# A hybrid decoder block on one core: the conv sums' accumulating DMAs read the stored tiles, and the means and the output projection get fixed places

## The chip, the cores and the metric

The kernel runs on one core of one Trainium2 chip. The time is device microseconds of one execution on that core; three runs of the kernel before are at hand. Beside them there is one profiled execution with its trace. Lower is better. Differences of about 0.3% can be told from none.

The engines by their names in the profile: PE multiplies matrices (PEld is its weight loads), DVE and ACT work on vectors, POOL is the general one, SP issues most of the DMA transfers. Each engine takes its instructions in order; a waiting instruction holds everything behind it on its engine. SP's and POOL's DMA issues wait in the same way.

## The reference

The block has S = 1024 positions, D = 1024 channels, 8 heads and a feed-forward width of 2816, all in float32. What matters of it:

```python
h = rms_norm(x, attn_norm_w)
q, k, v, u, g = jnp.split(h @ w_in, splits, axis=-1)
...                                        # differential attention over q, k, v
y_a = a.reshape(B, S, ATTN_WIDTH) @ w_proj_attn
u_a, u_b = jnp.split(u, 2, axis=-1)
c = causal_depthwise_conv(u_a * jax.nn.sigmoid(u_b), conv_w, conv_b)   # width 31
c = jax.nn.silu(layer_norm(c, conv_ln_w, conv_ln_b))                  # over the channels
y_b = c @ w_proj_conv
g_a, g_b = jnp.split(jax.nn.sigmoid(g + gate_b), 2, axis=-1)
x = x + (g_a * y_a + g_b * y_b) @ w_out
h = rms_norm(x, ffn_norm_w)
gt, up = jnp.split(h @ w_gate_up, 2, axis=-1)
x = x + (jax.nn.silu(gt) * up) @ w_down
```

The LayerNorm needs, at every position, the mean over all 1024 channels. The kernel gets the sum over the channels in two steps: the eight channel tiles of 128 channels are added up elementwise, and one matrix product with a constant tile adds over the 128 rows that are left.

## The kernel before

**Precision.** Each matrix product is made of three: both operands are split into a high part (a cast on ACT, `split_hi`, L120) and a low part (the rest, a subtraction on DVE, `split_lo`, L125), and high x high, high x low and low x high are added in PSUM (`mm3`, L168 to L170). So each weight tile of 128 x 1024 costs a DMA into a raw buffer, a cast and a subtraction before PE may use it.

**Stages.** One input projection makes Q, K, V, U and G. Attention works head by head; in its gaps PE computes gate columns (L168 to L170 on `pg`). The convolution runs on DVE in the background of all that. Behind attention come the LayerNorm, the projections of both branches, the gated merge, the output projection and the feed-forward part.

**The convolution.** `conv_taps(c)` lists the steps of channel tile c (128 channels x 1024 positions): the first tap on ACT (L576) writes `acc`, thirty taps on DVE (L582) add to it, one per step. There is one buffer `acc` (for the first four tiles a PSUM tile, copied into one SBUF buffer `done` at the end). After the last tap SP stores the tile to `c_d[c]` in DRAM (L588), and POOL issues a DMA that adds the same buffer to `cs_d` in DRAM (L590, `accum_op=ALU.add`); the first tile is stored there plainly (L592). The steps lie in a list `bg`, from which the other stages take so many at a time; `bg.until(0)` takes the rest.

**LayerNorm and what lies around it.** `ln_chunks(sb)` works on one half of the positions: SP loads the sums (`lns`, L1537) and the eight tiles (`cT_lo`), ACT and DVE split the sums into `lnmh` and `lnml`, two matmuls with `part` give the mean (L1545), then DVE subtracts it from each tile (L1551). It is a generator; `ln_both` walks through both halves, and `ln_step()` takes as many steps as the list `lnp` says, between column groups of the projection of the attention branch. That projection's first group, `o3`, is eight k-tiles x two columns x two halves in four PSUM banks; `ya_out` multiplies each bank with its sigmoid gate (L1618, DVE `gt`), and after that the bank is free for the next group. `early` (L1474) loads attention results back for it, `aTh` and `aTl` are their two parts.

**Output projection.** It runs as seven products of half size (`WSEVEN`, index z; j counts the four k-steps, i the four row tiles, each with three matmuls), whose operands are sums and differences of quarters of the weights, made by `wless` (L1750, DVE) and split by `wsplit`. After each product its four banks are added to the rows `xa` (L1824, DVE). A product's operand may be split ahead of time by `early_weights`. `norm2` (L1709 to L1717) normalizes rows that are complete, transposes them on PE (`tr`) and copies them back; `NORMS` says after which product and step this stands. Then the feed-forward part begins with the columns that `ws.plan` lists.

**What sets the order.** The program is written in one order, and a scheduler with a model of the engines' times then lists each engine's instructions; it may let an instruction slip ahead of others. `with after(ins)` keeps what is issued inside behind the instruction `ins` in that listing. Buffers come from pools with a fixed number of places; a new tile waits until the last reader of the old one is done.

## Time and profile before

| | us |
|---|---|
| three runs | 1749.77, 1753.22, 1754.83 |
| median of the runs | 1753.22 |
| the profiled execution's own time | 1750.81 |
| its span in the trace | 1749.0 |
| its mean granted TensorE clock | 0.998 |

The prediction is worked out against the profiled execution and carried over to the median. In the rows, a time at the left is the start in us from the span's beginning, then the duration, the engine, the line of the kernel, the operation, `out<-in` by the names in the program, the form, and in brackets how long the engine had stood before it and what ended that. Lists of waits say engine, line, what it waited for, and then total us, number of times, and the longest. Rows of windows give, after the length, the busy us (and instructions) of PE, PEld, DVE, ACT and POOL, the granted clock, the mean busy share of the 16 DMA engines, and GB/s.

### The profile page before, as it was taken

What the parts mean: (1) busy time and instruction counts of PE and PEld (TensorE: products, weight loads), DVE (VectorE), ACT (ScalarE), POOL (GpSimd) and SP (SyncE); (2) the same over time, 40 slices, a digit from 0 to 9 for tenths busy, and PEclk for the clock granted to TensorE, in tenths of its full rate; (3) what the DMA queues carried; (4) which work ended last, traced back from release to release, by engine and by line L of the source; (5) the groups of instructions that cost most, each with busy time, mean ns of one, the idle gap of its engine ahead of it and who ended that gap; (6) DMA issues with size and microseconds to landing.
All of it is one profiled execution on the core that took longest, in us unless ns stands there. A gap on an engine that the chain in (4) does not pass through costs nothing. (4 is left out here: it accounts for less than half of the span.)

```text
span 1749.0 us, 25887 instructions
## 1 busy us (share of the span) xinstructions
PE 1719.7 (98%) x9245; PEld 1480.1 (85%) x9245; DVE 1273.7 (73%) x2128; ACT 860.9 (49%) x1958; POOL 217.5 (12%) x207
## 2 busy tenths in 40 slices
PE   9999999999999999999899999999999999999999
PEld 7997889998998998988788877788888888888887
DVE  7575889797987888978587677866667666565554
ACT  5333335666777776755466324633333333333332
POOL 4987761000000000000000000000000000000000
PEclk9999999999999999999999999999999999999999
DMA  6343555334345344443873673235545544598663
GB/s 204 116 134 124 170 175 150 112 87 131 107 123 143 100 119 118 112 132 123 309 254 121 205 264 134 79 103 165 167 147 167 172 152 144 165 358 290 217 218 131
DMA packets 257765, 281.64 MB, mean 161 GB/s; under 512 B 16418, under 2 KB 178274, under 8 KB 257636
## 3 DMA queue, kind: packets, MB, share of 16 engines
q1 hardware_dynamic: 254352, 269.55, 47.7%
q0 software_dynamic: 2992, 9.39, 2.3%
q8 instruction: 73, 1.20, 0.3%
q10 hardware_dynamic: 292, 1.05, 0.2%
q14 instruction: 56, 0.46, 0.1%
HBM read 178.17 MB, written 85.50 MB: 151 GB/s over the span
## 5 line engine op out<-in xcount | busy, mean ns | idle before, releaser
L582 DVE SCALAR_TENSOR_TENSOR acc<-u,cw,acc 128x1023 f32<-128x1023 f32 (+14 forms) x240 | 303.9, 1266 | 17.1 <-ACT acc L576 14.7
L168 PE MATMUL pg<-whi,hT_hi 128*128 128x256 f32 x704 | 199.6, 285 | 2.0 <-ACT jk L787 2.0
L169 PE MATMUL pg<-wlo,hT_hi 128*128 128x256 f32 x704 | 200.4, 285 | 0.9 <-POOL wlo L131 0.9
L170 PE MATMUL pg<-whi,hT_lo 128*128 128x256 f32 x704 | 199.7, 284 | 0.0
L125 DVE TENSOR_TENSOR wlo<-draw,whi 128x1024 fp32r<-128x1024 f32 x75 | 91.8, 1224 | 85.6 <-ACT whi L120 78.1
L120 ACT CAST whi<-draw 128x1024 fp32r<-128x1024 f32 x75 | 79.1, 1055 | 129.5 <-PE acc L482 121.0
L168 PEld LDWEIGHTS pg<-whi,hT_hi 128*128 128x128 f32 x704 | 134.1, 191 | 4.6 <-ACT jk L787 2.7
L169 PEld LDWEIGHTS pg<-wlo,hT_hi 128*128 128x128 f32 x704 | 134.3, 191 | 3.0 <-POOL wlo L131 1.1
L170 PEld LDWEIGHTS pg<-whi,hT_lo 128*128 128x128 f32 x704 | 134.3, 191 | 1.2
L120 ACT CAST whi<-wraw 128x1024 fp32r<-128x1024 f32 x90 | 94.3, 1050 | 60.2 <-PE pg L169 26.4
L482 PE MATMUL acc<-wlo,whi 128*128 128x512 f32 x308 | 119.9, 389 | 0.0
L482 PE MATMUL acc<-whi,wlo 128*128 128x512 f32 x308 | 119.9, 389 | 0.0
L1282 ACT ACTIVATE E<-E,mn 128x640 f32<-128x640 f32 (+7 forms) x128 | 99.6, 779 | 39.5 <-DVE mn L1277 37.4
L168 PE MATMUL pg<-hT_hi,whi 128*128 128x512 f32 x288 | 114.8, 399 | 3.0 <-ACT jk L787 3.0
L170 PE MATMUL pg<-hT_hi,wlo 128*128 128x512 f32 x288 | 114.2, 397 | 0.0
L169 PE MATMUL pg<-hT_lo,whi 128*128 128x512 f32 x288 | 114.0, 396 | 0.0
L120 ACT CAST whi<-s 128x1024 fp32r<-128x1024 f32 x54 | 56.8, 1052 | 107.3 <-PE acc L967 101.1
L125 DVE TENSOR_TENSOR wlo<-wraw,whi 128x1024 fp32r<-128x1024 f32 x75 | 92.8, 1239 | 13.7 <-ACT whi L120 13.5
L1277 DVE CUSTOM_DVE_ANT_0 E<-sc,tb 128x512 f32<-128x512 f32 (+3 forms) x128 | 74.8, 588 | 31.5 <-PE pT L1314 15.1
L967 PE MATMUL acc<-h_hi,whi 128*128 128x512 f32 x240 | 93.4, 389 | 0.0
L967 PE MATMUL acc<-h_lo,whi 128*128 128x512 f32 x240 | 93.4, 389 | 0.0
L967 PE MATMUL acc<-h_hi,wlo 128*128 128x512 f32 x240 | 90.2, 389 | 0.0
(371 smaller groups left out, 4590.4 us busy)
## 6 DMA issues: line engine op xcount, KB each, us to landing
wraw<-in_w_gate_up_dram SPq DMA_DIRECT2D x44, 512.0 KB, 4.7
wraw<-in_w_in_dram SPq DMA_DIRECT2D x40, 512.0 KB, 4.5
qs<-qs SPq DMA_DIRECT2D x96, 128.0 KB, 2.3
wd<-in_w_down_dram SPq DMA_DIRECT2D x44, 256.0 KB, 3.1
tdT<-wd SPq DMA_DIRECT2D x88, 128.0 KB, 4.7
draw<-sdS SPq DMA_DIRECT2D x44, 256.0 KB, 4.0
draw<-tdT SPq DMA_DIRECT2D x44, 256.0 KB, 4.0
wraw<-in_w_in_dram SPq DMA_DIRECT2D x32, 256.0 KB, 3.3
```

The source lines that it names most:

```text
L120: act.copy(dst, src)
L125: last_lo[0] = dve.tensor_tensor(dst, src, f32(hi), op=ALU.subtract).ins
L168: pe.matmul(o, lh, rh, start=start, stop=False)
L169: pe.matmul(o, lh, rl, start=False, stop=False)
L170: last_mm[0] = pe.matmul(o, ll, rh, start=False, stop=stop).ins
L482: m = pe.matmul(o[s_][i][:], l_[:, ts], r_[:, 512:], start=start and j + y_ == 0, stop=j == n - 1 and y_ == 2, skip_group_check=not start,)
L582: dve.scalar_tensor_tensor(a_, us[c][:, : S - n], cw[:, c, t : t + 1], a_, op0=ALU.mult, op1=ALU.add)
L967: last_mm[0] = pe.matmul(o[:], a_[x_][:, k, :], b_[y_][:, k, :], start=start and k + x_ + y_ == 0, stop=k == 3 and x_ == 1, skip_group_che ...
L1277: dve.tensor_tensor_reduce(e[:, ks], o[:, :w], tb[:, S - nk + c0 : S - nk + c0 + w], 1.0, mn[:, j : j + 1] if c0 else 3.0e38, ALU.add, ALU ...
L1282: act.activation(e[:, :nk], e[:, :nk], AF.Exp, bias=mn[:, j : j + 1], scale=-1.0, accum_out=l[:, j : j + 1])
```

## The change

It has three parts.

First, the accumulating DMA of tile c reads the stored tile `c_d[c]` in DRAM instead of the buffer, in pieces of 1 KB (512 pieces of 256 elements instead of 128 of 1024), and is written at tap 15 of the next tile (behind DVE's last instruction there); the last tile's comes after the rest of the list.

Second, the LayerNorm's means: `ln_chunks` stops once more ahead of the mean's matmuls in the first half, and the step that issues them is written behind the seventh k-tile of the first group `o3`; the eighth k-tile's matmuls come after the last of them. The next step is placed behind the first gates.

Third, the output projection: every matmul of it comes after the one written before it; the weight sums of "22" and "S3" and their early splits are written at steps j == 1 of the fourth and j == 2 of the fifth product instead of at their starts; the loads of the first two gate/up columns are issued at the start of the sixth product; the norms of the third and fourth row tile are written one step later.

```diff
@@ ld_cols
-        def go():
-            raw = wraw()
+        raw = []
+
+        def load():
+            raw.append(wraw())
             nc.sync.dma_start(
-                raw[:].rearrange("p (k c) -> p k c", c=P),
+                raw[0][:].rearrange("p (k c) -> p k c", c=P),
...
+        def go():
+            if not raw:
+                load()
+            hi, lo = wsplit(raw[0], tiles)
...
+        go.load = load
         return [go]
@@ the convolution
+    def add_tile(c):
+        pool.dma_start(cs_d[:], c_d[c][:], accum_op=ALU.add, max_dma_last_dim=1024)
...
                     nc.sync.dma_start(c_d[c][:], acc[0][:])
-                    if c:
-                        pool.dma_start(cs_d[:], acc[0][:], accum_op=ALU.add)
-                    else:
+                    if c == 0:
                         nc.sync.dma_start(cs_d[:], acc[0][:])
+                if c > 1 and t == CW // 2:
+                    with after(last_of(mybir.EngineType.DVE)):
+                        add_tile(c - 1)
...
     bg.until(0)
+    add_tile(NKT - 1)
@@ the LayerNorm
+        if not sb:
+            yield
         for s_ in (s1h, s1l):
-            pe.matmul(mean[:], part[:], s_[:], start=s_ is s1h, stop=s_ is s1l)
+            last_mean[0] = pe.matmul(mean[:], part[:], s_[:], start=s_ is s1h, stop=s_ is s1l).ins
...
-        for z in (0, 1, 0, 0, 0, 1, 1, 0, 0, 0, 1, 1, 1, 1):
+        for z in (0, 0, 1, 0, 0, 0, 1, 1, 0, 0, 0, 1, 1, 1, 1):
...
-    lnp = [1, 3, 2, 2, 2, 2, 2, 9]
+    lnp = [1, 1, 3, 2, 2, 2, 2, 2, 9]
...
-                mm3(o3[c][sb][:], ...)
+                with after(last_mean[0]):
+                    mm3(o3[c][sb][:], ...)
+        if k == NKT - 2:
+            with after(last_mm[0]):
+                ln_step()
     for c in range(NE):
         ya_out(c, o3[c], g3[c])
-    ln_step()
+    with after(first_gates):
+        ln_step()
@@ the output projection
-    NORMS = {(5, 3): (0, 1), (6, 0): (2,), (6, 1): (3,)}
+    NORMS = {(5, 3): (0, 1), (6, 1): (2,), (6, 2): (3,)}
...
-        if z == 3:
-            for q in range(2):
-                room["22", q] = wraw()[:]
-            with after(last_lo[0]):
-                wless("22", "12", "S2")
-            for q in range(2):
-                early_weights("22", q, 2 * q)
-            wless("S3", "S4", "S3")
-        if z == 4:
-            for j in (2, 3):
-                early_weights("S3", j, 2 * j)
...
+            if z == 3 and j == 1:
+                for q in range(2):
+                    room["22", q] = wraw()[:]
+                with after(last_lo[0]):
+                    wless("22", "12", "S2")
+                    wless("S3", "S4", "S3")
+                for q in range(2):
+                    early_weights("22", q, 2 * q)
+            if z == 4 and j == 2:
+                for q in (2, 3):
+                    with after(last_lo[0]):
+                        early_weights("S3", q, 2 * q)
+            if z == 5 and j == 0:
+                with after(last_of(mybir.EngineType.SP)):
+                    for step in plain_first:
+                        step.load()
...
-                    with after(last_mm[0] if z == 6 else None), after(last_tr[0]):
+                    with after(last_mm[0]), after(last_tr[0]):
...
-                with after(last_mm[0]), after(last_add if z == 6 else None):
+                with after(last_mm[0]), after(last_add if z == 6 else None), after(norm_lo if z == 6 else None):
                     norm2(t_, r2[0], tr_first)
+                if z == 5:
+                    norm_lo = last_lo[0]
```

What stands in the engines' rows at three of the places follows. Numbers behind names tell tiles apart; they shift by one or two between the two programs.

POOL around the last tile's add, at the end of attention. Before:

```order
L1305 MEMSET pl_9598 128x128
L1304 MEMSET ph_9597 128x128
L590 DMA cs_d<-acc_8106 128x1024
L1305 MEMSET pl_9713 128x128
L1304 MEMSET ph_9712 128x128
L1512 MEMSET part 128x128
```

After:

```order
L1319 MEMSET pl_9598 128x128
L1318 MEMSET ph_9597 128x128
L1319 MEMSET pl_9712 128x128
L1318 MEMSET ph_9711 128x128
L579 DMA cs_d<-c_d_147 512x256
L1527 MEMSET part 128x128
```

The add has moved behind the last pair of memsets and reads the stored tile.

PE at the end of the first group `o3` (four banks `pg_`), where the mean's two matmuls stand (`lnmh`, then `lnml`); the next group is `pg_10229`. Before:

```order
L168 MATMUL pg_9986<-aTh_9763,whi_9632 128x512
L169 MATMUL pg_9986<-aTl_9769,whi_9632 128x512
L170 MATMUL pg_9986<-aTh_9763,wlo_9633 128x512
L1545 MATMUL mean_9954<-lnml_9956,part 128x512
L168 MATMUL pg_9988<-aTh_9763,whi_9776 128x512
L169 MATMUL pg_9988<-aTl_9769,whi_9776 128x512
L170 MATMUL pg_9988<-aTh_9763,wlo_9777 128x512
L168 MATMUL pg_10229<-aTh_9758,whi_9975 128x512
```

After, with the four banks' twelve matmuls of the eighth k-tile behind the means (the first ones shown):

```order
L169 MATMUL pg_9986<-aTl_9910,whi_9776 128x512
L170 MATMUL pg_9986<-aTh_9908,wlo_9777 128x512
L1564 MATMUL mean_9954<-lnmh_9955,part 128x512
L1564 MATMUL mean_9954<-lnml_9956,part 128x512
L168 MATMUL pg_9983<-aTh_9763,whi_9631 128x512
L169 MATMUL pg_9983<-aTl_9769,whi_9631 128x512
L170 MATMUL pg_9983<-aTh_9763,wlo_9632 128x512
L168 MATMUL pg_9984<-aTh_9763,whi_9631 128x512
```

The low half of the mean has gone from three matmuls before the group's end to twelve.

PE in the output projection, from the second product (banks `wo_11566` to `wo_11569`) to the third (`wo_11646` to `wo_11649`); `wo_11498` to `wo_11500` are banks of the first product's kind, used again by the fourth. Before:

```order
L1814 MATMUL wo_11569<-whi_11530,mTl_10793 128x512
L1814 MATMUL wo_11498<-whi_11650 128x512
L1814 MATMUL wo_11499<-whi_11650 128x512
L1814 MATMUL wo_11500<-whi_11650 128x512
L1814 MATMUL wo_11646<-whi_11570,mTh_10782 128x512
L1814 MATMUL wo_11646<-wlo_11571,mTh_10782 128x512
L1814 MATMUL wo_11646<-whi_11570,mTl_10788 128x512
L1814 MATMUL wo_11646<-whi_11570,mTh_10784 128x512
```

After:

```order
L1843 MATMUL wo_11569<-whi_11530,mTl_10793 128x512
L1843 MATMUL wo_11646<-whi_11570,mTh_10782 128x512
L1843 MATMUL wo_11646<-wlo_11571,mTh_10782 128x512
L1843 MATMUL wo_11646<-whi_11570,mTl_10788 128x512
L1843 MATMUL wo_11647<-whi_11570,mTh_10782 128x512
L1843 MATMUL wo_11647<-wlo_11571,mTh_10782 128x512
L1843 MATMUL wo_11647<-whi_11570,mTl_10788 128x512
L1843 MATMUL wo_11648<-whi_11570,mTh_10782 128x512
```

The three matmuls of the fourth product are gone from ahead of the third, and the third goes from bank to bank at each step instead of finishing one bank first.

More of the change, by code (lines that the diff above doesn't have):

```diff
@@ L295, in ld_cols @@
     def ld_cols(w, c0, tiles=wtiles):
-        def go():
-            raw = wraw()
+        raw = []
+        def load():
+            raw.append(wraw())
             nc.sync.dma_start(
-                raw[:].rearrange("p (k c) -> p k c", c=P),
+                raw[0][:].rearrange("p (k c) -> p k c", c=P),
                 w[:, c0 : c0 + P].rearrange("(k p) c -> p k c", p=P),
             )
-            hi, lo = wsplit(raw, tiles)
+        def go():
+            if not raw:
+                load()
+            hi, lo = wsplit(raw[0], tiles)
             return (
@@ L550 @@
     for f in range(NSTD):
-        ws.plan(ld_cols(wgu, f * P) + ld_cols(wgu, FF + f * P, *([fourth] if f == 1 else [])))
+        plain = ld_cols(wgu, f * P) + ld_cols(wgu, FF + f * P, *([fourth] if f == 1 else []))
+        ws.plan(plain)
+        if f == 0:
+            plain_first = plain
     cv_ctx = ExitStack()
@@ L1524 @@
     cT_lo = big.tile([P, NKT, S], F32R, tag="xlo", name="cT_lo")
+    last_mean = [None]
     def ln_chunks(sb):
@@ L1635 @@
                 cs = slice(sb * 512, (sb + 1) * 512)
-                mm3(o3[c][sb][:], w3[c][0][:, k, :], w3[c][1][:, k, :], aT_hi[k][:, cs], aT_lo[k][:, cs], k == 0, k == NKT - 1)
+                with after(last_mean[0]):
+                    mm3(o3[c][sb][:], w3[c][0][:, k, :], w3[c][1][:, k, :], aT_hi[k][:, cs], aT_lo[k][:, cs], k == 0, k == NKT - 1)
+        if k == NKT - 2:
+            with after(last_mm[0]):
+                ln_step()
     for c in range(NE):
         ya_out(c, o3[c], g3[c])
-    ln_step()
+    with after(first_gates):
+        ln_step()
     for c in range(NE, NKT):
```

## The prediction

> **What bounds the kernel now.** I read the page's busy times first, then PE's list of waits, then the rows of each wait, then who is late there.
>
> ```profile
> PE 1719.7 (98%) x9245; PEld 1480.1 (85%) x9245; DVE 1273.7 (73%) x2128; ACT 860.9 (49%) x1958; POOL 217.5 (12%) x207
> ```
>
> PE is busy for 1719.7 of 1749.0 us. The change takes no matmul away, so all that it can win lies in some 29 us in which PE stands, plus what the granted clock loses after a stand. The list of PE's waits (line, releaser: us in total, times, longest) gives the largest:
>
> ```profile
> PE pg L168 <- ACT jk L787: 4.9, 4, 3.0
> PE tr L1712 <- ACT xa L1717: 2.7, 1, 2.7
> PE pg L168 <- DVE gt L1618: 2.5, 1, 2.5
> PE wo L1814 <- ACT whi L120: 1.8, 1, 1.8
> PE sc L1275 <- DVE mn L1277: 1.5, 2, 1.2
> ...
> PE sc L1275 <- DMA ks<-klo: 1.3, 1, 1.3
> ```
>
> The first and the last two are in the attention stage, the third at the LayerNorm's means, the others in the output projection: the three places that the change touches.
>
> **Part 1, the accumulating DMAs.** The first tap of a channel tile (L576, on ACT) writes into the one buffer that the add of the tile before (L590) still reads. These rows give what ACT waits for, when the tile's store (L588) and the add (L590) are issued, and how long they take to land:
>
> ```profile
>   DMA cs_d<-acc: 6.9, 3
>   DMA cs_d<-done: 2.1, 1
> ...
> L588 SPq DMA_DIRECT2D c_d<-acc x4: 320/332/344, 406.5 to 824.8; - x4
> DMA to landing us min/median/max: 2.9/4.5/5.3
> ...
> L590 POOL DMA_DIRECT2D cs_d<-acc x4: 863/864/873, 406.7 to 825.1; - x4
> DMA to landing us min/median/max: 7.4/9.0/10.0
> ```
>
> Afterwards the add reads the stored tile, so the first tap waits for the store alone, 3 to 7 us sooner. What that is worth is read at the places. The dearest:
>
> ```profile
> 413.11 0.19 ACT L787 ACTIVATION_READ_ACCUMULATOR jk<-pg 128x1 f32 x1
> 416.16 1.24 ACT L576 ACTIVATE acc<-u,pvec,cw 128x1024 f32<-128x1024 f32 x1 [2.86 <-DMA cs_d<-acc]
> ...
> 420.10 0.80 PE L168 MATMUL pg<-hT_hi,whi 128*128 128x512 f32 x1 [2.98 <-ACT jk L787]
> ...
> 420.00:423.00 3.00, 2.90 (x7) 2.35 (x8) 3.00 (x9) 2.54 (x7) 0.00 (x0) 0.50 0.21 80
> ```
>
> ACT is free at 413.3. The store was issued at 406.5 and landed by 411.8 at the latest (5.3), so the wait of 2.86 goes entirely. It is what holds back the squares (L787) that free PE's bank: PE's 2.98 goes with it. The last row (window; PE, PEld, DVE, ACT, POOL busy; granted clock; DMA share; GB/s) shows the clock at 0.50 for the 3 us behind the stand, which loses another 1.5 us. This place: 4.5 us.
>
> The second place goes through two engines:
>
> ```profile
> ACT acc L576 <- DMA cs_d<-acc: 2.2, 1, 2.2
> ...
> 559.70 0.17 DVE L1289 RECIPROCAL rl<-l 128x2 f32<-128x2 f32 x1 [4.25 <-ACT E L1282]
> ...
> 569.26 0.47 PE L1275 MATMUL sc<-ks,qs 128*128 128x512 f32 x1 [1.34 <-DMA ks<-klo]
> 575.69 0.33 PE L1275 MATMUL sc<-ks,qs 128*128 128x128 f32 x1 [1.15 <-DVE mn L1277]
> ```
>
> ACT's 2.2 (until 557.0) makes the exponentials late, DVE stands 4.25, its klo is late, and the DMA from it and the scores behind it are what PE waits for. Both PE waits, 1.34 + 1.15 = 2.5 us, are smaller than or about as large as the 2.2 removed at the head; I take them whole. Of ACT's four waits two are left (6.9 + 2.1 - 2.9 - 2.2 = 3.9 us); PE shows only small stands behind them, so I price both at 1.0, between 0 and 3.9. Part 1 gives 4.5 + 2.5 + 1.0 = 8.0 us; ends 7.0 and 10.9.
>
> The add's own price: it moves behind a tap in the middle of the next tile, on POOL behind a pair of memsets. The next pair waits for PE, near the second place for this long:
>
> ```profile
> POOL pl L1305 <- PE pW L170: 16.8, 1, 16.8
> ```
>
> The add has 512 pieces instead of 128, so 0.86 us of issue becomes at most four times that, 3.5: hidden under 16.8, and 2.6 each if that cover were gone. Nothing on SP stands behind an add except at the last tile (below). But the placing of the rest is remade: the orders of PE differ from row 1039 on, so every small stand of the attention stage is dealt anew. I price that at 0, ends -3 and +3.
>
> **Part 2, the means, and the loads ahead of them.** The add of the last tile shares the DMA engines with loads that PE waits for. Rows of PE, then ACT's wait, then the window:
>
> ```profile
> 836.79 0.50 PE L168 MATMUL pg<-aTh,whi 128*128 128x512 f32 x1 [0.76 <-ACT aTh L120]
> 838.05 0.50 PE L169 MATMUL pg<-aTl,whi 128*128 128x512 f32 x1 [0.76 <-DVE aTl L125]
> 839.19 0.50 PE L168 MATMUL pg<-aTh,whi 128*128 128x512 f32 x1 [0.41 <-ACT sgg L626]
> ...
> ACT aTh L120 <- DMA early<-a_d: 4.3, 2, 2.2
> ...
> 836.00:843.00 7.00, 5.07 (x14) 3.48 (x14) 5.28 (x8) 5.78 (x13) 0.00 (x0) 0.76 0.55 187
> ```
>
> The three stands are 1.93 us, and a clock of 0.76 over 7 us loses 1.7 more: 3.6 in all. Afterwards the add, issued at 825.1 before, waits for the store that went out at 824.8, so its packets come some 4 us later (2.9 to 5.3), behind most of these loads. I take 2.0, the stands without the clock's loss, since the add then meets the next loads instead; ends -0.6 (the add lands on another such load and costs a stand of the sizes seen) and +3.6.
>
> The means. In the order shown the mean's second half (lo) stands three matmuls ahead of the group's end, and on DVE four subtractions from the mean stand ahead of the gating (L1618) that frees PE's banks:
>
> ```profile
> 864.85 0.51 PE L168 MATMUL pg<-aTh,whi 128*128 128x512 f32 x1 [2.50 <-DVE gt L1618]
> ...
> 861.71 0.69 DVE L1551 TENSOR_TENSOR lnd<-cT_lo,mean 128x512 f32<-128x512 f32 x1 [5.01 <-PE mean L1545]
> ...
> 864.11 2.48 DVE L1618 TENSOR_TENSOR gt<-pg,gt 128x512 f32<-128x512 f32 x4
> ...
> 865.00:870.00 5.00, 5.00 (x22) 4.09 (x23) 5.00 (x7) 2.08 (x3) 0.00 (x0) 1.00 0.97 354
> ```
>
> PE's last matmul before the stand ends at 864.85 - 2.50 = 862.35. A matmul takes 5.00 / 22 = 0.227 us (last row). Afterwards 12 of them (2.72) follow the mean, so it ends at 859.6, and the four subtractions (861.71 to 864.11, 2.4 us) are over at 862.1. The gating then starts at 862.35 and its first quarter (2.48 / 4 = 0.62) frees a bank at about 863.0. Of 2.50 some 0.6 is left: gain 1.9, ends 0 and 2.5.
>
> SP asks for the sums at 842.73 in this program, with the tile and gate loads behind that request. The last add, issued by 824.8 + 5.3 = 830, lands after 7.4 to 10.0 (the rows above), at 837 to 840: nothing is held. The nearest copy from DRAM to DRAM is no slower:
>
> ```profile
> t_d<-b_d POOLq DMA_DIRECT2D x8, 576.0 KB, 5.7
> ...
> 842.73 0.81 SPq L1537 DMA_DIRECT2D lns<-cs_d  x1
> ```
>
> Adding and four times the pieces may stretch it; up to 12 it is still free.
>
> **Part 3, the output projection in the program's order.** Rows of PE, DVE and ACT:
>
> ```profile
> 1043.77 0.96 PE L1814 MATMUL wo<-whi 128*128 128x512 f32 x3 [1.18 <-DVE xa L1824]
> 1063.11 1.22 PE L1814 MATMUL wo<-whi 128*128 128x512 f32 x4 [1.80 <-ACT whi L120]
> 1097.07 1.14 PE L1712 MATMUL tr<-ident,xa 128*128 128x128 f32 x8 [2.69 <-ACT xa L1717]
> ...
> 1041.87 3.08 DVE L1824 TENSOR_TENSOR xa<-wo,xa 128x512 f32<-128x512 f32 x5
> 1044.86 1.22 DVE L125 TENSOR_TENSOR wlo<-room,whi 128x1024 fp32r<-128x1024 f32 x1
> ...
> 1095.49 1.04 ACT L120 CAST whi<-wraw 128x1024 fp32r<-128x1024 f32 x1 [1.88 <-DMA wraw<-in_w_gate_up_dram]
> ...
> 1094.00:1100.00 6.00, 3.31 (x19) 2.53 (x18) 3.98 (x7) 4.46 (x8) 0.00 (x0) 1.00 0.16 49
> ```
>
> New waits. PE ends the second product at 1043.77 - 1.18 = 1042.6 and may no longer slip three matmuls of the fourth product in; it goes on when the fourth addition (0.6 each from 1041.87) is done, 1044.4: a stand of 1.8 in place of 1.18. The third bank's addition comes only behind the wlo of 1044.86 and two more, at 1047.3, where PE is after six matmuls, 1045.8: another 1.5. In the fifth product a low half stands behind eight weight sums and two low halves that were moved there; by their number (8 x 0.62, 4 x 1.2) PE waits 0 to 2.0, I take 1.5. Gone: the 1.80 (with the strict order the splits are far ahead when that product starts), and the 2.69: 24 matmuls (5.4 us) now come between the transposes of the first two and of the third row tile, and the wait of 1.88 of ACT's split falls behind the copies that free the banks. Sum: 1.18 - 1.8 - 1.5 + 1.80 - 1.5 + 2.69 = 0.9, ends +5.7 (no new wait) and -2.4 (of the 2.69 only 1.0 is gained, and the clock's drop costs 1.6). The two gate/up loads that are issued earlier, behind the stores of x, cost nothing while SP's queue is short of work there.
>
> Would the clock drop at 1042 to 1047? In the rows it dropped behind one stand of 2.98, and behind three of 0.76, 0.76 and 0.41, and not behind the 2.69 (clock 1.00 in the last row). Two stands of 1.8 and 1.5 lie between; I charge nothing and keep 1.6 for the range. By the Trainium skill, "TensorE: Matmul & The Clock Gate", Part 1, the clock falls to half after an idle window of about 3.4 us, and no single gap over that is to be left. By that rule neither this place nor the one at 417 would have lost anything; the trace halves the clock after 2.98 us, so the row decides.
>
> **The sum.** 8.0 + 2.0 + 1.9 + 0.9 = 12.8 us. The profiled run took 1750.8 (span 1749.0 and 1.8 around it), so 1738.0; the median of the runs shown is 2.4 above that run: 1740.4.
>
> **Rivals.**
> - The reshuffled attention stage takes the gain of part 1 back: ACT, free 3 us sooner, meets a late load or DVE instead. For it: DVE waited 4.3 for a table load at 574.93 and its order is new everywhere. Against it: the stage has few stands besides those named. Then only 2.0 + 1.9 + 0.9 are left: 1748.4, and 1752.9 if one new stand is as dear as the 4.5 at 417.
> - The adds are slow, and it ends slower. If each of the 512 pieces costs what one of the 128 does now, the last add lands 30 to 40 us after its issue at 830, at 860 to 870. SP's request for the sums stands until then, with the tile and gate loads behind it; PE needs the gates at 862, and they came with some 6 us to spare, so beyond a landing at 849 each microsecond is PE's. It decides from about 12.8 later, 862: at 870 the loss is 21 and the time 1753.2 - 12.8 + 21 = 1761.4. Against it: nothing in the rows says that a piece's cost doesn't fall with its size. By an estimate from the Trainium skill, "DMA: Bandwidth & Descriptors", Why small descriptors are slow, with 3 cycles on top of 32-byte beats, four pieces of 1 KB take 140 cycles where one of 4 KB takes 131; by that the landing would stay near 10 us. No run here shows it yet.
> - The loads at 836 gain nothing, as the add only moves onto the next ones: 1742.4 to 1743.0.
> - The change doesn't do what it says: the first tap then waits for the store or its own input just as long, and the time stays at 1748.4 to 1753.
>
> **Chances.** My forecast 0.62, the reshuffled stage 0.18, the loads 0.10, the slow adds 0.07, no effect 0.03. The forecast's own range is 1733 to 1747 (ends of the terms, not all at once). For 8 in 10 I take 1731 to 1756: all of the gains at their upper ends below, and above the reshuffled stage with one or two dear new stands. 0.3% is 5.3 us, about what can be told from no change: faster than 1748 comes from the forecast (0.59), the loads (0.09) and a part of the reshuffled stage (0.04), 0.72; within, 0.03 + 0.09 + 0.01 + 0.03 = 0.16; slower, 0.05 of the reshuffled stage, 0.06 of the slow adds and 0.01 besides, 0.12.
>
> **What would show it.** Right: no wait of the first tap's ACT line on the sums' DMA; no stand of PE near 417 and no clock of 0.5 there; gates at the means waited for under 1 us; stands of 1 to 2 us at the second and third bank of the third product; no stand at the first transposes. Wrong: SP's request for the sums standing beyond 849, new stands of 2 us or more in the attention stage, or a clock of 0.5 in the output projection.

## The result and the profile after

The changed kernel takes 1740.09 us (median of 6 runs, 1738.69 to 1742.06), the kernel before beside it 1752.89 (6 runs, 1748.93 to 1754.83). The ratio is 0.9932, 95% interval 0.9918 to 0.9946: faster by 12 to 13 us. The profiled execution has a span of 1737.0 us against 1749.0. Forecast were 1740.4 us and 12.8 us less.

The page's busy times and the list of PE's waits of the changed kernel, the largest and those that answer to the lines shown before:

```profile
PE 1717.4 (99%) x9245; PEld 1478.8 (85%) x9245; DVE 1275.2 (73%) x2128; ACT 863.3 (50%) x1958; POOL 218.6 (13%) x207
...
PE acc L981 <- POOL wlo L131: 4.0, 1, 4.0
PE wo L1843 <- DVE xa L1855: 3.1, 2, 1.9
PE wo L1843 <- DVE wlo L125: 1.6, 1, 1.6
...
PE pg L168 <- DVE gt L1637: 0.5, 1, 0.5
```

The squares' waits (4.9), the one for klo (1.3) and the first transposes' (2.7) are gone; the gates' has gone from 2.5 to 0.5. New are the 4.0 for POOL's wlo, which was 1.0 before, and the three in the output projection.

Where the 12 us came, stage by stage, is read from the same matmul in both traces. Two rows of before that were not shown, the last attention step and the first matmul of the feed-forward part:

```profile
827.76 0.36 PE L168 MATMUL pW<-ph,vh 128*128 128x256 f32 x1
...
1107.55 0.47 PE L168 MATMUL pg<-h_hi,whi 128*128 128x512 f32 x1 [0.26 <-DVE xa L1824]
```

and the rows of the changed kernel, with PE's first matmul behind the gates between:

```profile
821.69 0.36 PE L168 MATMUL pW<-ph,vh 128*128 128x256 f32 x1 [0.15 <-DVE pl L125]
853.22 0.50 PE L168 MATMUL pg<-aTh,whi 128*128 128x512 f32 x1 [0.46 <-DVE gt L1637]
1095.48 0.47 PE L168 MATMUL pg<-h_hi,whi 128*128 128x512 f32 x1 [0.71 <-DVE xa L1855]
```

| stage | from the rows | gained, us | forecast |
|---|---|---|---|
| up to the last attention step | 827.76 to 821.69 | 6.1 | 8.0 |
| loads, to PE's arrival at the gates | 862.35 to 852.76, less 6.07 | 3.5 | 2.0 |
| the gates | 2.50 to 0.46 | 2.0 | 1.9 |
| output projection | 1107.55 to 1095.48, less 11.63 | 0.4 | 0.9 |

The sum is 12.0, the difference of the spans. The adds themselves (issue and landing of L579), what the first tap (L589) still waits for, and SP's request for the sums:

```profile
L579 POOL DMA_DIRECT2D cs_d<-c_d x7: 1006/1031/1101, 205.7 to 823.4; - x7
DMA to landing us min/median/max: 6.1/8.6/11.4
...
  DMA c_d<-done: 3.1, 1
  DMA c_d<-acc: 1.3, 1
...
835.89 0.37 SPq L1554 DMA_DIRECT2D lns<-cs_d  x1
```

Four times the pieces cost POOL 1.03 us instead of 0.87, and they land as soon as before. The first tap waits 4.4 us in two for stores instead of 9.0 in four for sums. The last add, issued at 823.4, has landed by 834.8 at the latest, ahead of SP's request.

### The profile page after: what moved, and what is told of

It is laid out like the page before. It is cut to its first block, busy times and chain, and to the rows that moved or that the text cites. A ratio compares the mean times of both kernels' runs of the same rounds, so it can differ in the third digit from the quotient of the medians.

```text
span 1737.0 us, 25860 instructions
## 1 busy us (share of the span) xinstructions
PE 1717.4 (99%) x9245; PEld 1478.8 (85%) x9245; DVE 1275.2 (73%) x2128; ACT 863.3 (50%) x1958; POOL 218.6 (13%) x207
## 4 chain that ended last, share of the span: by engine, by line
PE 89%; DVE 4%; DMA 3%; ACT 2%; POOL 1%; issue 1%; SPq 0%; POOLq 0%
PE acc L981 28%; PE acc L489 12%; PE pg L168 12%; PE pg L169 11%; PE pg L170 11%; PE wo L1843 2%; PE sc L1290 2%; PE sc L1289 2%; PE pT L1328 2%; DVE acc L595 1%; PE pW L168 1%; PE pW L169 1%; PE pW L170 1%; PE pg L1107 1%; DMA wraw<-in_w_in_dram 1%
```

## The experiments

**Part 1 alone.** The change's lines in the convolution and nothing else.

```diff
+    def add_tile(c):
+        pool.dma_start(cs_d[:], c_d[c][:], accum_op=ALU.add, max_dma_last_dim=1024)
...
+                if c > 1 and t == CW // 2:
+                    with after(last_of(mybir.EngineType.DVE)):
+                        add_tile(c - 1)
```

> Part 1 alone (the adds read the stored tiles, 15 taps later; means and output projection as before). Theory: the attention stage and the loads at 836 are part 1's, so the span falls from 1749.0 to about 1739.5 (6 us up to the last attention step, 3.5 us at the loads and the half clock there), the first tap waits for no sums DMA, PE has no stand at 417, 569 and 576, and the 4.0 us stand on POOL's wlo near 230 is there as in the changed kernel, since PE's rows are the same as there up to the first group o3. The stands of 2.5, 1.2, 1.8 and 2.7 at the means and in the output projection stay. Rival (the fixed places carry the gain): the span stays above 1744 and the loads at 836 keep their three stands.

Measured: 1744.42 us, ratio to before 0.9969 (0.9958 to 0.998), span 1743.1. Its waits of PE and, as windows, the gates and the place that follows the third product:

```profile
PE acc L971 <- POOL wlo L131: 3.6, 1, 3.6
PE tr L1717 <- ACT xa L1722: 2.7, 1, 2.7
PE pg L168 <- DVE gt L1623: 2.5, 1, 2.5
PE wo L1819 <- ACT whi L120: 1.8, 1, 1.8
...
854.34 0.80 PE L168 MATMUL pg<-aTh,whi 128*128 128x512 f32 x1 [2.49 <-DVE gt L1623]
...
853.00:858.00 5.00, 3.66 (x10) 2.91 (x11) 5.00 (x8) 3.58 (x6) 0.00 (x0) 0.66 1.02 394
1053.00:1059.00 6.00, 5.00 (x14) 3.79 (x15) 6.00 (x6) 1.42 (x2) 0.00 (x0) 0.72 0.08 24
```

Every wait is where it was expected: none at 417, 569 and 576 to speak of, the stand at POOL's wlo, the four old ones behind. PE arrives at the gates at 854.34 - 2.49 = 851.85, 10.5 us before the old kernel, 1.0 more than forecast (6 + 3.5). But the span is 3.6 us above the 1739.5: the clock fell to half behind three of the old stands (the windows' 0.66 and 0.72 instead of 1.00, and a third at 1089), where in the profile of before the same stands, 2.50, 1.80 and 2.69, were followed by full clock; by PE's rows that costs 4.6 us in all. So part 1's time alone understates it; its stage is confirmed, the sum was not.

**Part 2 alone.** The lines of the LayerNorm.

```diff
-    lnp = [1, 3, 2, 2, 2, 2, 2, 9]
+    lnp = [1, 1, 3, 2, 2, 2, 2, 2, 9]
...
+                with after(last_mean[0]):
+                    mm3(o3[c][sb][:], ...)
```

> Part 2 alone. Theory: attention has the rows of before, so all its stands stay (2.98 near 417, half clock behind it, 1.34, 1.15, and three at the loads); only the stand at the gates behind the means goes from 2.5 to about 0.5: span 1747.0. Rival (the means' gain hangs on the earlier loads or on the later add): with the loads late as before, SP's queue and ACT are late too, the gate stand stays above 1.5 us and the span above 1748.

Measured: one run, 1750.53 us, span 1748.8. The gates' wait:

```profile
863.18 0.50 PE L168 MATMUL pg<-aTh,whi 128*128 128x512 f32 x1 [0.45 <-DVE gt L1622]
...
1094.00:1100.00 6.00, 4.81 (x18) 4.12 (x19) 2.43 (x4) 4.72 (x9) 0.00 (x0) 0.72 0.02 3
```

2.50 has become 0.45 with the loads as late as before, which rules out the rival's mechanism. That the span fell by 0.2 us only has two other causes. PE arrives at the gates 0.4 us later than in the old kernel's profile (863.18 - 0.45 = 862.73), as some stands of the attention stage were longer in this execution. And the stand at the first transposes is followed by half clock (0.72 in the window, 1.00 in the same window before), which costs 1.5 us by PE's rows.

**Part 3 alone.** The lines of the output projection and of `ld_cols`.

```diff
-                    with after(last_mm[0] if z == 6 else None), after(last_tr[0]):
+                    with after(last_mm[0]), after(last_tr[0]):
```

> Part 3 alone. Theory: the output projection trades stands: 1.9, 1.2 and 1.6 come, 1.2, 1.8 and 2.7 go; span 1748.5, within 1 us of before, and every row ahead of it as before. Rival (the strict order only pays because the stages ahead end earlier): the new stands are larger here, 6 us or more together, and the span is 1750 or more.

Measured: one run, 1755.47 us, span 1753.7.

```profile
PE wo L1829 <- DVE xa L1841: 2.8, 2, 1.9
PE wo L1829 <- DVE wlo L125: 1.6, 1, 1.6
...
1044.00:1056.00 12.00, 9.19 (x28) 6.55 (x27) 6.50 (x10) 3.72 (x9) 0.00 (x0) 0.72 1.04 410
```

The stands are near those forecast (1.9, 0.9 and 1.6, where 1.9, 1.2 and 1.6 were expected). But the window shows a clock of 0.72 over 12 us: two stretches of half clock follow the pair, where the changed kernel's profile has 1.00 (below). By its time the rival's 1750 was exceeded, by its stands the theory held; the difference is the clock, here and behind the gates (a wait of 2.5 as before), and 1 us that the stages ahead of the gates took longer in this execution. Part 3 as it is brings nothing by itself and carries a risk of some us.

**The old kernel without the adds.**

```diff
-                    if c:
-                        pool.dma_start(cs_d[:], acc[0][:], accum_op=ALU.add)
-                    else:
+                    if c == 0:
                         nc.sync.dma_start(cs_d[:], acc[0][:])
```

> The kernel before with the accumulating DMAs of tiles 1 to 7 left out (the sums then hold the first tile alone). Theory: what part 1 wins is the wait for these DMAs and their traffic at the loads, so without them the time up to the last attention step and the loads at 836 is that of part 1 alone within about 2 us: span 1738 to 1741, first tap waiting only for the store, early loads landing 2 to 3 us sooner. Rival (the waits only move to the store or the input of the next tile; the gain comes from the new order): the first tap still waits 9 us in all, or the loads at 836 still land after 9 to 10 us.

Measured: one run, 1735.34 us, span 1733.6: better than expected. PE has no stand at 417, 569, 576, at the loads (which land after 5.5 us at the latest), and none at 230 either. So the waits for the adds, and their packets at the loads, are what the old kernel paid for. PE arrives at the gates at 847.85 - 2.49 = 845.4 us here, at 852.76 in the changed kernel: that one still pays 7.4 us for its adds up to there, 5.4 of it near 230 (a stand of 4.00 where there is none here, and some 1.4 of clock behind it, worked out below). PE's order is the same in both up to about 690 us, well past that place, but the weights that POOL sums for the product at 230 come 4 us earlier:

```profile
213.43 1.29 POOL L946 TENSOR_TENSOR s<-wraw 128x512 f32<-128x512 f32 x1 [5.47 <-DMA wraw<-in_w_in_dram]
...
847.85 0.50 PE L168 MATMUL pg<-aTh,whi 128*128 128x512 f32 x1 [2.49 <-DVE gt L1616]
```

(217.53 in the changed kernel, shown further down). So with the order of the changed kernel and without the adds there is no stand at 230: the suspect is the first add's traffic, not the order alone.

**The last add as before.**

```diff
+                    if c == NKT - 1:
+                        pool.dma_start(cs_d[:], acc[0][:], accum_op=ALU.add)
...
-    add_tile(NKT - 1)
```

> The changed kernel, but the last tile's add as before: from the buffer acc, issued with the store and not after it. PE's rows are those of the changed kernel up to the end of the first group. Theory: the add's packets meet the early loads again; these land after 8 to 10 us instead of 6.2, PE has two or three stands of 0.4 to 1.0 us there again, and with the clock's loss behind them 2.0 to 3.6 us are lost against 1737.0: 1739 to 1740.6. Rival (the loads come sooner because attention ends more smoothly, not because the add is out of their way): landing stays near 6.2 us and the span within 1 us of 1737.0.

Measured: one run, 1746.06 us, span 1744.3. The early loads, PE's waits there, and the windows of the loads and of the third product:

```profile
DMA to landing us min/median/max: 6.1/9.0/9.8
...
PE pg L168 <- ACT aTh L120: 0.9, 1, 0.9
PE pg L169 <- DVE aTl L125: 0.8, 1, 0.8
...
830.00:838.00 8.00, 5.95 (x18) 3.98 (x17) 4.98 (x6) 6.08 (x13) 0.00 (x0) 0.79 0.56 210
1035.00:1046.00 11.00, 7.98 (x23) 5.66 (x22) 5.99 (x10) 3.72 (x9) 0.00 (x0) 0.69 1.03 409
```

With nothing changed but this add, the loads land after 9.0 us (median; 6.2 in the changed kernel), the stands of 0.9 and 0.8 are back, and the half clock behind them: 0.9 + 0.8 + 8 x 0.21 = 3.4 us at the loads, the theory's upper end. The rest of the 7.3 us is elsewhere: the half clock behind the third product (0.69), and one stand of 1.5 us at a late load of q in attention, at a place where the changed kernel has none. One run doesn't tell whether these belong to the edit.

**Pieces of 256 bytes.**

```diff
-        pool.dma_start(cs_d[:], c_d[c][:], accum_op=ALU.add, max_dma_last_dim=1024)
+        pool.dma_start(cs_d[:], c_d[c][:], accum_op=ALU.add, max_dma_last_dim=256)
```

> The changed kernel with the adds in 2048 pieces of 256 bytes instead of 512 of 1 KB. All engines' rows are the same. From 128 to 512 pieces POOL's issue went from 0.87 to 1.03 us and the landing from 9.0 to 8.6 us. Theory (a piece costs little beside its bytes): issue under 2 us, landing under 15 us, nothing waits for it, span 1737 within 1 us. Rival (each piece has a price of its own, which shows once there are enough): landing 25 us or more; the last add, issued at 823.4, then lands at 848 or later, SP's request for the sums (835.9) and the gate loads behind it stand, and PE stands at the means or the gates: span 1743 or more.

Measured: one run, 1738.7 us, span 1736.9.

```profile
L579 POOL DMA_DIRECT2D cs_d<-c_d x7: 1806/1828/1903, 205.3 to 823.8; - x7
DMA to landing us min/median/max: 7.4/10.0/13.2
```

POOL's issue grows by 0.80 us for 1536 more pieces, 0.5 ns a piece; the median landing grows by 1.4 us. The forecast's rival with adds that cost per piece is out: with sixteen times the old number of pieces the last add, issued at 823.8, landed by 837.0 at the latest (13.2), where SP's request stood at 835.9 in the changed kernel; that is far from the 849 at which it would decide.

**The weight sums earlier.** The stands that the strict order brought are DVE's sums and low halves ahead of the additions. This moves them to where DVE stands.

```diff
-            if z == 1 and j == 2:
+            if z == 1 and j == 1:
                 with after(last_lo[0]):
                     wless("S2", "S4", "S1")
-            if z == 3 and j == 1:
+            if z == 2 and j == 1:
...
-                with after(last_lo[0]):
+                with after(last_add):
                     wless("22", "12", "S2")
                     wless("S3", "S4", "S3")
...
-                with after(last_of(mybir.EngineType.DVE) if z == 6 else None):
+                with after(last_of(mybir.EngineType.DVE) if z == 6 else last_add if z == 2 else None):
                     hi, lo = ws.next()
```

> The changed kernel with the weight sums of the output projection placed where DVE stands: S2's at step 1 of the second product instead of step 2, those of 22 and S3 at step 1 of the third product, behind the additions of the second, and the split of the fourth product's first weights behind these additions too. PE's rows are the same. Theory: PE's stands of 1.90 and 1.22 at the third product and 1.58 in the fifth came from DVE's sums and low halves ahead of what PE needed; all three go or stay under 0.3 each: 4.0 to 4.7 us less, span 1732.5 and ratio to the changed kernel about 0.9975. Rival (PE needs the banks sooner than DVE can add at all, or the moved sums only push other low halves back): 2 us or more of stands remain, at the third product or behind it.

Measured: 1735.03 us (4 runs, 1733.57 to 1735.54), ratio to before 0.9914 (0.9899 to 0.9929), span 1733.3.

```profile
PE acc L981 <- POOL wlo L131: 3.2, 1, 3.2
...
PE wo L1844 <- DVE xa L1856: 0.9, 2, 0.4
...
1028.00:1040.00 12.00, 11.14 (x48) 8.44 (x48) 11.22 (x17) 6.32 (x12) 0.00 (x0) 1.00 1.03 413
```

Of 1.90 + 1.22 + 1.58 there are 0.9 left, and the clock has nothing to fall behind. By PE's rows the output projection is 4.4 us shorter, and 0.7 us were lost ahead of it, so the span falls by 3.7. The theory holds: DVE's order ahead of the additions was the cause.

**The product order near 230 kept.** The same with a placement in the input projection's last U tile (`last_s3` is the last matmul of the tile before's product S3).

```diff
+        with after(last_s3[0] if c in (7,) else None):
+            product(b, A["11"], B[0, 0], True)
...
+        with after(last_s3[0] if c in (7,) else None):
+            product(a, A["12"], B[1, 0], True)
```

> The same with the first two products of the last U tile placed behind the third sum's product of the tile before it. In the listing this also changes the order near 230, where PE in the changed kernel took the second product's low half before the twelve matmuls of another tile and stood 4.0 us on POOL's wlo. Theory: with those twelve matmuls (2.7 us) ahead again the stand there is 1.0 to 1.6 us, without the half clock behind it: 3 to 4 us less than the kernel with the sums earlier, about 1729, if the attention stage, whose order is dealt anew, stays as it was. Rival (what the listing gives there it takes elsewhere): the stands of the attention stage grow by 2 us or more, and the span stays above 1731.

Measured: 1733.33 us (4 runs, 1732.29 to 1736.17), ratio to before 0.991 (0.9894 to 0.9927), span 1731.1.

```profile
229.28 0.50 PE L981 MATMUL acc<-hT_hi,wlo 128*128 128x512 f32 x1 [0.69 <-POOL wlo L131]
...
PE sc L1293 <- DMA ks<-klo: 2.2, 1, 2.2
```

POOL's wlo is done at the same time (229.3; 229.9 in the changed kernel), and PE stands 0.69 instead of 4.00, because matmuls of another tile run ahead. So PE's order can hide the late low half; it did so in the old kernel, where the same sums were as late (217.64). Why they are late it doesn't say. What the order gives there it takes in part elsewhere: klo's DMA is late and PE stands 2.2 at 563, with a half clock behind it. The stand at 230 went as the theory had it; the span of 1731.1 is what the rival gave.

**The changed kernel and this one side by side.**

> The changed kernel once more, beside the next one and the kernel before on one chip. What is asked: whether its pair of stands at the third product (1.90 and 1.22) is followed by a half clock in some executions and not in others. It was followed by none in the changed kernel's profile, by one stretch of about 3.4 us with 256-byte pieces, and by two in part 3 alone and with the last add as before. Theory (the clock looks at the time in stretches of its own, which these stands meet by chance): runs spread over 3 us or more, profile between 1736 and 1741, ratio to before 0.992 to 0.996. Rival (a fixed threshold, the drops in the other kernels have other causes): runs within 1.5 us of each other.

> The kernel with the sums earlier and the product order kept, in the same call as the changed kernel. Theory: the stands that it lacks (1.90, 1.22 and 1.58 in the output projection, some 3 of the 4.0 near 230, and the half clocks that may follow them) are worth 6 to 8 us against the changed kernel, less about 3 us for the later DMA of klo at 563: 4 to 6 us, ratio to the changed kernel 0.9965 to 0.998. Rival (the order dealt anew gives all of it back): less than 2 us.

Measured on one chip: the changed kernel 1738.55 us (5 runs, 1738.40 to 1740.62), ratio to before 0.9931 (0.9918 to 0.9945); the kernel with both edits 1735.16 (4 runs, 1733.60 to 1736.85), ratio to before 0.991 (0.9896 to 0.9923). Between the two medians lie 3.4 us, less than the 4 to 6 expected: in this profile of the second the stand at 563 was 4.0 us.

The pair of stands in the output projection, in windows of equal length: the changed kernel's first profile, then its second.

```profile
1030.00:1041.00 11.00, 7.88 (x34) 5.89 (x33) 6.21 (x10) 4.61 (x10) 0.00 (x0) 1.00 1.04 411
```

```profile
1030.00:1041.00 11.00, 8.90 (x33) 6.49 (x32) 5.76 (x9) 4.70 (x10) 0.00 (x0) 0.84 1.04 410
```

The same program has a full clock in the one and one stretch of half clock in the other. It cost some 0.4 us only by PE's rows (33 matmuls done against 34 in the window): the first half-speed matmuls used up what the second stand would have been. The expected spread of 3 us or more did not come, and the rival's 1.5 was exceeded: 2.2, with four of the five runs within 0.3.

**The add's place held on POOL.** In the changed kernel the add is written 15 taps into the next tile, behind the last DVE instruction. But DVE's order doesn't hold a DMA that POOL issues: written right behind the store instead, the add leaves the rows of all five engines as they are in the scheduler's listing. The trace shows it, too. The first add went out at 205.68, when DVE was at its 4th tap of that tile, and stands on POOL ahead of the weight sums that start at 217.53. Rows of POOL:

```profile
205.68 1.10 POOL L579 DMA_DIRECT2D cs_d<-c_d  x1
...
217.53 1.29 POOL L962 TENSOR_TENSOR s<-wraw 128x512 f32<-128x512 f32 x1 [8.33 <-DMA wraw<-in_w_in_dram]
```

This puts it behind the last instruction of POOL:

```diff
                 if c > 1 and t == CW // 2:
-                    with after(last_of(mybir.EngineType.DVE)):
+                    with after(last_of(mybir.EngineType.Pool)):
                         add_tile(c - 1)
```

> The changed kernel with the adds placed behind POOL's last instruction at tap 15 instead of DVE's. With DVE's, POOL's rows are the same as when an add is written right behind its store, and in the changed kernel the first add went out at 205.7, during the fifth tap of the next tile. In the kernel without adds a weight load issued at 205 landed 4 us sooner and PE had no stand near 230, though PE's rows there are those of the changed kernel. Theory: the first add's packets, 206 to 216, delay that load, POOL's low half behind it and so PE. With the add behind POOL's work at 222 the load lands after about 7 us, POOL's sums start at 213.5 and PE has no stand there: 4.7 us less, span 1732 to 1733. Rival (the load is late for another reason): POOL's sums start at 217 as before.

Measured: one run, 1734.96 us, span 1733.2. Four microseconds while the load is under way, as a window of the changed kernel; then, of this one, POOL's rows, the same window and that at 230:

```profile
212.00:216.00 4.00, 4.00 (x20) 3.30 (x19) 3.96 (x5) 1.31 (x2) 0.00 (x0) 1.00 1.06 179
```

```profile
213.66 1.30 POOL L962 TENSOR_TENSOR s<-wraw 128x512 f32<-128x512 f32 x1 [6.08 <-DMA wraw<-in_w_in_dram]
...
219.89 1.05 POOL L579 DMA_DIRECT2D cs_d<-c_d  x1
...
212.00:216.00 4.00, 4.00 (x19) 3.31 (x18) 3.96 (x5) 2.42 (x4) 2.27 (x2) 1.00 0.18 55
...
229.00:233.00 4.00, 4.00 (x19) 3.31 (x18) 3.93 (x5) 1.60 (x2) 3.37 (x3) 1.00 0.34 101
```

The add now goes out at 219.9, behind the sums. The load is there 4 us sooner (the DMA engines are busy for 0.18 of the window instead of 1.06), POOL's sums start at 213.7 as without any add, and PE has no stand at 230. The theory held: the 4.0 came from the first add's packets in the way of a weight load. PE's order is also dealt anew here, so this run alone doesn't separate its part at 230; the kernel without the adds does, which has the changed kernel's order there, the sums at 213.43 and no stand. Of the 4.7 us expected the span gained 3.8: the new order has a stand of its own (1.8, below), and the clock fell behind the pair in the output projection.

**Both edits that gained.** The add's place on POOL and the weight sums earlier.

> The same with the weight sums of the output projection earlier. Theory: the gains add, 1737.0 - 4.7 - 3.8 = 1728.5 in span, 1730 in time, as long as the adds, now really in mid tile, meet no load that PE waits for; ratio to before about 0.988. Rival (each add meets other loads there): new stands on klo, q or the tables in attention of 2 us or more, span above 1731.

Measured: 1730.58 us (4 runs, 1729.93 to 1731.42), ratio to before 0.9891 (0.9872 to 0.9909), span 1728.1. Its largest waits of PE:

```profile
PE pQ L816 <- DVE qkraw L808: 1.8, 1, 1.8
PE pm L209 <- DVE busy L196: 1.5, 1, 1.5
```

It came out as expected (1728.5 in span, 1730), and it is faster than both kernels: 1749.19 was the old one beside it, and the changed kernel's interval (0.9918 to 0.9946) lies wholly above this one's; 0.0041 between the ratios are some 7 us. The first of these waits is new with the add's place (also 1.8 in the run before).

## Why the prediction was right

- **Part 1, the first tap** (8.0, ends 7.0 to 10.9). The waits at 417, 569 and 576 went, as worked out, and so did the half clock behind the first: 7.0 us. The two smaller waits of the first tap, priced at 1.0, were worth some 0.7: behind ACT's 2.06 at 316.48 and 1.80 at 704.67 PE stood 0.28 and 0.39. So this term was right, mechanism and size.

- **The order dealt anew** (0, ends -3 and +3). This is the step that failed, though its net of about -1.7 lies within the ends: it lost 4.4 at one place and won about 2.7 at others, and I had priced neither. The loss, near 230, is 4.00 - 1.04 = 3.0 of stand and 1.4 of clock: seven matmuls take 3.1 us in the window below (clock 0.57), and 1.7 in the kernel before, where the clock is full.

```profile
229.00:233.00 4.00, 3.10 (x7) 2.48 (x8) 3.66 (x3) 0.00 (x0) 3.18 (x2) 0.57 0.56 163
```

The gain lies at stands of the kernel before that were not in the sum, with no wait of the first tap in the 60 us ahead of them; of the 4.9 us on the squares the prediction had priced the 2.98 alone:

```profile
281.55 1.09 PE L802 MATMUL pQ<-ident,qkraw 128*128 128x128 f32 x8 [0.70 <-DVE qkraw L794]
302.06 0.39 PE L169 MATMUL pg<-wlo,hT_hi 128*128 128x256 f32 x1 [0.93 <-POOL wlo L131]
391.14 0.39 PE L168 MATMUL pg<-whi,hT_hi 128*128 128x256 f32 x1 [1.39 <-ACT jk L787]
```

These and one of 0.30 at 378.79 are gone in the new order, and one of 0.61 at 305.54 is new. In the two kernels with the add's place held on POOL, whose order is another, most of them are back (1.8 on `pQ`, 0.7 and 0.6 on POOL's wlo, 0.5 on the squares), which speaks for the order as their cause. The stage's 6.1 is thus about 7.6 - 4.4 + 2.7. Of the loss I said that PE's rows differ from 1039 on and left it at that; read there, they show a product that waits for POOL's low half moved ahead of twelve matmuls that don't, and POOL's time for that low half stood in the trace. The cause behind it was there before as well: the first add's packets delay a weight load by 4 us, of which the old order of PE hid 3. I looked for the adds' cost on ACT and at the last tile only, and took the 15 taps at their word without reading where the early adds stand on POOL.
- **The loads** (2.0, ends -0.6 and 3.6). 3.5 measured, 3.4 by undoing this alone. The mechanism was right; I should have taken the clock's loss with the stands, as the add's later packets met nothing that PE waited for.
- **The means** (1.9). 2.04 in the change and 2.05 alone.
- **The last add and SP** (free up to a landing 12 us behind its issue). Landed within 11.4.
- **The output projection** (0.9). 0.4. The three new stands were forecast as 1.8, 1.5 and 1.5 and came as 1.90, 1.22 and 1.58; the old ones of 1.80 and 2.69 went; and the first matmul of the feed-forward part waits 0.71 instead of 0.26, which was not in the sum. That the clock stayed full behind the new pair, as charged, was luck: the same program's second profile had a stretch of half clock there, and part 3 alone and the last add as before had two, which cost 2.5 us in the latter.
- **The rivals.** The reshuffled stage took 4.4 back and gave 2.7, so it was a part of the truth rather than a case of its own. The slow adds are ruled out by the pieces.

The median came out within 0.3 us of the forecast, and the gain of the spans, 12.0, within 0.8. Partly this was luck, as errors of opposite sign met: 2.7 for the stands that the new order removed and 1.5 for the loads were not counted, and neither were the 4.4 at 230.

## What to carry to other kernels

A buffer that a slow DMA reads is released when that DMA lands; letting the slow one read a copy that a fast one has stored anyway frees the buffer sooner and costs only traffic, which should be kept away from loads that the busiest engine waits for. Such a place holds only if it is fixed on the engine that issues the DMA (here POOL); fixed on another, it did nothing. Where a change makes a scheduler list the rows anew, look at the first row that differs and ask what it waits for in the old trace, before pricing the rest at nothing. An order that is fixed on one engine paid here only when an engine that feeds it was ordered for it too: the fixed places in the output projection brought 0.4 us, and some 3.8 us more of stands went once DVE's sums stood where DVE was idle.

## What the runs showed of the hardware

The price of a stand on PE is not its length. A stand of 2.5 us at the gates was followed by full clock in the kernel before and by half clock for some 3.4 us in part 1 alone (the 0.66 of the window at 853 above), with the same matmuls around it; the pair of 1.9 and 1.2 did either, too (1.00 and 0.84 above), and a single stand of 1.8 in part 1 alone was enough (0.72). How much it costs differs as well: behind the pair, one stretch of half clock lengthens matmuls that would have stood anyway, and little is lost.

The traces show what decides. By their records of the clock, the stretches of half clock of one trace lie on one grid of 3.413 us: those of the kernel before start at 419.71 and 839.55, 123 steps apart, three of part 1 alone at 854.06, 1055.44 and 1089.58, 59 and 10 steps apart. What counts is how much of one such step PE stood, and the same stand can fall into one step or be split between two. The stand at the gates, in the two steps of the kernel before and in the one of part 1 alone that ends where the half clock starts:

```profile
860.03:863.44 3.41, 2.32 (x11) 1.58 (x9) 1.73 (x3) 0.95 (x2) 0.00 (x0) 1.00 0.17 65
863.44:866.86 3.42, 2.02 (x9) 1.65 (x10) 3.42 (x7) 3.42 (x6) 0.00 (x0) 1.00 0.95 370
```

```profile
850.64:854.06 3.42, 1.21 (x6) 0.67 (x4) 2.85 (x5) 2.07 (x4) 0.00 (x0) 1.00 1.01 388
```

PE stood 1.1 and 1.4 us of the first two and 2.2 of the third. The pair of 1.9 and 1.2 is the same: 0.7 and 1.8 in two steps of the changed kernel's first profile, 1.9 in one of its second. With 256-byte pieces even a stand of 3.1 us, at 229, was split into 1.25 and 1.86 and followed by full clock. Over the 14 traces here, from full clock: where PE stood 1.9 us or more of a step, 22 times, half clock followed each time; with 1.4 to 1.86 it followed in 4 of 18; with less it never did. So the bound lies near half a step; PE's ends are modelled in these traces, which may blur it.

The Trainium skill, "TensorE: Matmul & The Clock Gate", Part 1, says that the clock looks at activity in windows of 3413 ns that run freely, without regard to the kernel. The grid agrees with that. That a whole idle window is needed, as the same section has it, does not agree: 1.9 us within a window always sufficed.

An accumulating DMA of 512 KB in 128, 512 or 2048 pieces landed after 9.0, 8.6 and 10.0 us (medians), the first read from SBUF and the others from DRAM: neither four times the pieces and the other source together nor four times the pieces again changed it much. By the fit in the Trainium skill, "DMA: Bandwidth & Descriptors", Anatomy of one DMA, of 2.0 us and bytes over 436 GB/s, an estimate would be 3.2 us; the section doesn't speak of accumulating, and the measurement decides here. One such add in flight made a weight load of the same size land 4 us later.
